# Rows of cumulated gates: spread over the partitions by DMA and masked on GpSimd, instead of by products on TensorE

## The chip, the cores and the metric

The kernel runs on one core of a Trainium2 chip. The metric is the device time of one execution in microseconds (us); three runs of the kernel before took 2589.52, 2592.03 and 2594.63 us, so the median is 2592.03 us. The engines are called as in the profile: PE (TensorE, matrix products), DVE (VectorE), ACT (ScalarE), POOL (GpSimd) and SP (SyncE, which here issues the weight loads).

## The reference

The model has two residual layers over 256 tokens of width 2048. The first mixes by centred means, the second by a gated delta rule in both directions; each has a cross-attention to 256 memory tokens, a SiLU gate and an output projection. What the change touches is in the second layer: the decay between two tokens of a chunk, for each of 32 heads and 2 directions, and its use in the triangular matrix and in the attention inside a chunk.

```python
g = jnp.cumsum(g.reshape(b, h, n, c), axis=-1)
tril = jnp.tril(jnp.ones((c, c), bool))
strict = jnp.tril(jnp.ones((c, c), bool), -1)
diff = g[..., :, None] - g[..., None, :]
decay = jnp.where(tril, jnp.exp(jnp.where(tril, diff, 0.0)), 0.0)
lower = jnp.where(strict, jnp.einsum('bhnid,bhnjd->bhnij', k_beta, k) * decay, 0.0)
a_mat = lower + jnp.eye(c, dtype=lower.dtype)
attn_intra = jnp.where(tril, jnp.einsum('bhnid,bhnjd->bhnij', q, k) * decay, 0.0)
```

## The kernel before

All dense products stream their weights: 802 tiles of 512 KB are loaded by SP into the buffers `wr` (`fetch`, line 208; `W_RAW_BUFS` of them), ACT makes the rounded high half `wh` (line 218), DVE the low half `wl` by a subtraction (line 220), each in one of three split buffers, and PE makes three products for each piece (high times high, high times low, low times high), into a bank called `pd`. `take` asks for the split of the tiles that come three later and for the loads that come `W_RAW_BUFS` after those. A tile's raw buffer is free when its subtraction has ended, a split buffer when PE has used the tile.

PE and SP issue in the order in which the class `Flow` writes the program. It keeps an estimated time `now`, adds to it for every product (in `mm`), and at each step of a dense job looks whether a chain (a Python generator that yields how long the other engines will need) is due; if so, the chain's next instructions are put there. DVE, ACT and POOL are ordered by a scheduler at build time, by priorities and by what is ready; each works through its own queue strictly in order.

The delta-rule layer has eight groups of four value heads. `group_chain(g)` makes, for each of two key heads, the gram matrix `kk` of the keys on PE, and then for its two value heads and two directions a pass:

- the cumulated gates of that head and direction, a row of 384 numbers (three blocks of 128 tokens), are spread over all 128 partitions by a product of a column of a selection matrix `selr` with `rows` (which holds the rounded value and its remainder in its two halves of the partitions); a second product, the identity `identr` with `maskr`, adds -1e30 where the decay has to vanish, in the first and the third block;
- ACT takes the exponentials of the sum with the bias `ngc` out of the PSUM bank `pa` into `Ap` (lines 936 and 937);
- DVE multiplies them with `kk` and a scalar into `U` (lines 940 and 945);
- the generator yields `Y_UA`.

Eight passes make a group, 64 the program. Afterwards DVE eliminates inside small blocks (lines 993 and 999, on `Ti`, whose start values POOL loads at line 913), PE puts the blocks together, `solve_pair` makes the outputs, and `norm_chain` and the gates finish the group while the next one's passes begin. `Ap` and `U` have one buffer each, so the passes of a group follow the last products that read the `Ap` of the group before.

`decay_chain` runs once, before the groups: it computes the gates, their cumulated rows `rowf` (64 heads and directions by 384), and splits them into `rows`. At the start of the program `mem_tiles` issues the first weight loads and the eight loads of the memory in turn, `fetch(c + 1 if c < W_RAW_BUFS else W_RAW_BUFS)` ahead of each.

Of the kernel before, what the change touches and what calls it, by code (L numbers as in the profile page):

```python
# [9 lines left out]
F32 = mybir.dt.float32  # L10
F32R = mybir.dt.float32r
I32 = mybir.dt.int32
AF = mybir.ActivationFunctionType
ALU = mybir.AluOpType
# [3 lines left out]
P = 128  # L18
S = 256
D = 2048  # L20
KT = D // P
# [5 lines left out]

# buffers per tag, and dense steps between two looks at the chains
W_RAW_BUFS = 4
W_SPLIT_BUFS = 3  # L30
PS_DENSE = 3
PS_CHAIN = 3
CHAIN_BUFS = 6
SQ_BUFS = 3
SLICE = 2
# priorities of the weight staging and of the parts of a chain on ScalarE and VectorE
P_STAGE = 600
P_UA = 600
P_INV = 600
P_NORM = 600  # L40
# how long the tensor engine leaves a step of a chain to the other engines, in units of US ns
US = 1300.0
# [20 lines left out]
CS_ID, CS_SEL, CS_ONE, CS_MASK = 0, 128, 192, 194  # L63
# [19 lines left out]
class Flow:  # L83
    """Interleaves dense weight products with the dependent chains, in the order the tensor engine issues them."""

# [52 lines left out]
def trunk_kernel(  # L138
# [18 lines left out]
    nc = tc.nc  # L157
    V, A, T = nc.vector, nc.scalar, nc.tensor
    flow = Flow()

    keep = ctx.enter_context(tc.tile_pool(name="keep", bufs=1))
# [8 lines left out]
    def pa(n):  # L170
        t = psa.tile([P, 512], F32, tag="a", name="pa")
        return t[:, 0:n]

    def mm(out, lhsT, rhs, start=True, stop=True):
        n = 1
        for d in rhs.shape[1:]:
            n *= d
        if rhs.dtype == F32R:
            flow.now += n / 2.4 if n >= 256 else n * 1.7
        elif lhsT.shape[0] == P:  # L180
            flow.now += 4 * n / 2.4 + 4
        else:
            flow.now += 2 * n / 2.4 + 4
        T.matmul(out, lhsT=lhsT, rhs=rhs, start=start, stop=stop)  # L184
# [494 lines left out]

    identr = keep.tile([P, P], F32R, name="identr")  # L680
    selr = keep.tile([P, 64], F32R, name="selr")
    maskr = keep.tile([P, 2, P], F32R, name="maskr")
    cwh = small[:, SM_CW : SM_CW + 320].rearrange("p (c k) -> p c k", k=5)
    nwh = keep.tile([P, 1], F32, name="nwh")
    fsel = keep.tile([P, 4], F32R, name="fsel")
    rows = keep.tile([P, 384], F32R, name="rows")
    ngc = keep.tile([P, 2, 64], F32, name="ngc")
# [6 lines left out]
    def decay_chain(ps):  # L694
        mask = mp.tile([P, 2, P], F32, tag="ms", name="mask", bufs=KT)
        nc.gpsimd.dma_start(out=mask, in_=cst_d[:, CS_MASK:CS_W].rearrange("p (d m) -> p d m", d=2))
        V.tensor_copy(out=identr, in_=ident)
        V.tensor_copy(out=selr, in_=cst[:, CS_SEL : CS_SEL + 64])
        V.tensor_tensor(
            out=fsel, in0=cst[:, CS_SEL : CS_SEL + 4], in1=cst[:, CS_SEL + 32 : CS_SEL + 36], op=ALU.add  # L700
        )
        V.tensor_copy(out=maskr, in_=mask)
        V.tensor_scalar(
# [48 lines left out]
        A.copy(out=rowf, in_=rps[0:64])  # L752
        A.copy(out=rows[0:64], in_=rowf)
        V.tensor_tensor(out=rows[64:128], in0=rowf, in1=rows[0:64].bitcast(F32), op=ALU.subtract)
        yield 1.5
# [17 lines left out]

    # second part: the jobs of the delta-rule groups
    kqs = [[None] * 4 for _ in range(8)]
# [115 lines left out]

    prio = [0]

    def urgent(gen, offset):
# [8 lines left out]
    def group_chain(g):  # L903
# [18 lines left out]
        for i in range(2):  # L922
            kk = gram(i, kq[i])
            for h in (2 * i, 2 * i + 1):
                for d in range(2):
                    hd = d * 4 + h
                    hdg = d * 32 + 4 * g + h
                    ja, jb = d, 1 - d
                    ps = pa(384)
                    mm(ps, selr[:, hdg : hdg + 1].to_broadcast([P, P]), rows, True, False)  # L930
                    mm(
                        ps.rearrange("p (b m) -> p b m", b=3)[:, 0:3:2, :], identr,
                        maskr[:, d : d + 1, :].to_broadcast([P, 2, P]), False, True,
                    )
                    E = Ap[:, hd, :]
# [452 lines left out]
```

## Time and profile before

| | |
|---|---|
| runs (us) | 2589.52, 2592.03, 2594.63 |
| profiled execution: span (us) | 2590.5 |
| profiled execution: time outside the span | not given by the profile |
| PE busy | 2566.3 us, 99% |
| DVE busy | 1788.2 us, 69% |
| ACT busy | 1238.0 us, 48% |
| POOL busy | 15.5 us, 1% |
| mean granted clock of PE | 0.998 |
| read from HBM | 430.63 MB, 167 GB/s over the span |

An engine is busy while at least one of its instructions runs. PE's matmuls overlap each other, so the duration of one is longer than the distance to the next; what a matmul takes from PE is that distance. Waits are listed as who waited, on which line, and what ended the wait.

### The profile page before, as it was taken

How to read it: one execution, taken by the hardware profiler on the slowest of the kernel's cores; microseconds unless marked ns; L12 is line 12 of the kernel's file. 1: busy time of each engine (PE TensorE's matmuls, PEld its weight loads, DVE VectorE, ACT ScalarE, POOL GpSimd, SP SyncE). 2: the span in 40 equal slices, each digit the busy share in tenths (PEclk: the TensorE clock that was granted, in tenths of full speed). 3: DMA queues.
4: the chain of work that ended last, by engine and by line, in shares of the span. 5: the costliest groups of instructions: out<-in, count | busy, mean ns of one | idle time of the engine just before them, and what ended most of it. 6: DMA issues, size and time to landing. Idle time of an engine off the chain costs nothing.

```text
span 2590.5 us, 53005 instructions
## 1 busy us (share of the span) xinstructions
PE 2566.3 (99%) x21996; PEld 2510.7 (97%) x21996; DVE 1788.2 (69%) x3317; ACT 1238.0 (48%) x1946; POOL 15.5 (1%) x44
## 2 busy tenths in 40 slices
PE   8999999999999999999999999999999999999998
PEld 7899999999999999998999999999999999999998
DVE  6564455656557576674546557989889797979786
ACT  5444434434444443554344445555545555565544
POOL 0000000000000000000000000000000000000000
PEclk9999999999999999999999999999999999999999
DMA  7654455555555555655554545535344454535353
GB/s 241 219 185 160 159 172 166 184 185 187 184 185 187 184 185 187 204 190 189 190 186 156 164 161 167 167 116 164 127 155 136 138 163 133 164 127 166 125 175 103
DMA packets 120817, 436.17 MB, mean 168 GB/s; under 512 B 13728, under 2 KB 13984, under 8 KB 120576
## 3 DMA queue, kind: packets, MB, share of 16 engines
q1 hardware_dynamic: 118080, 426.06, 50.4%
q0 software_dynamic: 1776, 5.64, 0.7%
q8 instruction: 172, 2.82, 0.4%
q10 hardware_dynamic: 720, 1.08, 0.1%
q14 instruction: 69, 0.57, 0.1%
HBM read 430.63 MB, written 2.10 MB: 167 GB/s over the span
## 4 chain that ended last, share of the span: by engine, by line
PE 96%; DVE 2%; ACT 1%; issue 0%; DMA 0%; POOL 0%; DVEq 0%
PE pd L184 86%; PE pa L184 9%; PE kk L184 1%; DVE wl L220 1%; PE pa L188 0%; ACT wh L218 0%; DMA xs<-in_mem_dram 0%; DVE ms L348 0%; DVE o L1264 0%; DMA wr<-in_wv_dram 0%; DVE Dg L983 0%; DVE cacc L795 0%; DVE L L985 0%; ACT ms L347 0%; DVE itmp L993 0%
## 5 line engine op out<-in xcount | busy, mean ns | idle before, releaser
L220 DVE TENSOR_TENSOR wl<-wr,wh 128x1024 fp32r<-128x1024 f32 x802 | 981.1, 1223 | 609.1 <-ACT wh L218 607.2
L184 PE MATMUL pd<-xs,wh 128*128 128x256 f32 x7328 | 1351.4, 286 | 2.8 <-DVE gt L411 2.1
L218 ACT CAST wh<-wr 128x1024 fp32r<-128x1024 f32 x802 | 841.0, 1049 | 1043.3 <-PE pd L184 839.8
L184 PEld LDWEIGHTS pd<-xs,wh 128*128 128x128 f32 x7328 | 1143.5, 192 | 7.4 <-DVE gt L411 2.3
L184 PE MATMUL pd<-xs,wl 128*128 128x256 f32 x3664 | 1036.5, 283 | 0.0
L184 PEld LDWEIGHTS pd<-xs,wl 128*128 128x128 f32 x3664 | 702.1, 192 | 0.0
L184 PE MATMUL pd<-y,wh 128*128 128x256 f32 x2944 | 524.0, 280 | 1.1 <-DVE y L258 1.1
L184 PEld LDWEIGHTS pd<-y,wh 128*128 128x128 f32 x2944 | 449.7, 187 | 1.8 <-DVE y L258 1.3
L184 PE MATMUL pd<-y,wl 128*128 128x256 f32 x1472 | 410.7, 279 | 0.0
L184 PEld LDWEIGHTS pd<-y,wl 128*128 128x128 f32 x1472 | 276.6, 188 | 0.0
L184 PE MATMUL pd<-ms,wh 128*128 128x256 f32 x1536 | 271.4, 279 | 0.0
L184 PEld LDWEIGHTS pd<-ms,wh 128*128 128x128 f32 x1536 | 234.8, 188 | 0.2
L184 PE MATMUL pd<-ms,wl 128*128 128x256 f32 x768 | 214.9, 280 | 0.0
L184 PE MATMUL pd<-wh,ms 128*128 128x512 f32 x512 | 163.4, 398 | 6.2 <-ACT ms L347 6.2
L184 PEld LDWEIGHTS pd<-ms,wl 128*128 128x128 f32 x768 | 144.3, 188 | 0.0
L795 DVE SCALAR_TENSOR_TENSOR cacc<-cu,small,cacc 128x256 f32<-128x256 f32 x256 | 122.5, 482 | 5.7 <-ACT cacc L793 1.3
L184 PEld LDWEIGHTS pd<-wh,ms 128*128 128x128 f32 x512 | 96.7, 189 | 29.2 <-ACT ms L347 6.2
L447 DVE TENSOR_TENSOR xT<-xT,pd 128x512 f32<-128x512 f32 x140 | 95.8, 684 | 41.2 <-PE pd L184 41.0
L184 PE MATMUL pd<-wl,ms 128*128 128x512 f32 x256 | 102.0, 398 | 0.3 <-DVE wl L220 0.2
L993 DVE TENSOR_TENSOR itmp<-L,Ti 128x126 f32<-128x126 f32 (+22 forms) x248 | 62.6, 252 | 2.3
L999 DVE TENSOR_TENSOR Ti<-Ti,itmp 128x126 f32<-128x126 f32 (+22 forms) x248 | 62.7, 253 | 2.2
L257 ACT CAST y<-yf 128x256 fp32r<-128x256 f32 x92 | 35.9, 405 | 55.7 <-DVE yf L525 54.0
(217 smaller groups left out, 1778.5 us busy)
## 6 DMA issues: line engine op xcount, KB each, us to landing
wr<-in_dw_dram SPq DMA_DIRECT2D x258, 512.0 KB, 3.5
wr<-in_pw_dram SPq DMA_DIRECT2D x192, 512.0 KB, 3.5
wr<-in_wo_dram SPq DMA_DIRECT2D x192, 512.0 KB, 3.5
wr<-in_wv_dram SPq DMA_DIRECT2D x64, 512.0 KB, 3.6
wr<-in_wk_dram SPq DMA_DIRECT2D x64, 512.0 KB, 3.5
wr<-in_pg_dram SPq DMA_DIRECT2D x32, 512.0 KB, 3.5
xs<-in_mem_dram SPq DMA_DIRECT2D x8, 256.0 KB, 7.1
xT<-in_x_dram SPq DMA_DIRECT2D x4, 512.0 KB, 6.3
```

Of the source, the lines that this page charges most:

```text
L184: T.matmul(out, lhsT=lhsT, rhs=rhs, start=start, stop=stop)
L218: A.copy(out=hi, in_=raw)
L220: V.tensor_tensor(out=lo, in0=raw, in1=hi.bitcast(F32), op=ALU.subtract)
L257: A.copy(out=dst[:, 0, :], in_=src)
L447: V.tensor_tensor(out=xv, in0=xv, in1=pss[0], op=ALU.add)
L795: V.scalar_tensor_tensor(out=a, in0=u[:, k : k + S], scalar=cwh[:, ct, k : k + 1], in1=a, op0=ALU.mult, op1=ALU.add)
L993: V.tensor_tensor(out=tv, in0=L[:, j + 1 : 32, j : j + 1].to_broadcast([P, n, c]), in1=Ti[:, j : j + 1, 0:c].to_broadcast([P, n, c]), op=A ...
L999: V.tensor_tensor(out=Ti[:, j + 1 : 32, 0:c], in0=Ti[:, j + 1 : 32, 0:c], in1=tv, op=ALU.subtract)
```

## The change

The rows stay in float32 and are written once to DRAM, to `rows_d`, by a DMA from POOL. For each pass a DMA from POOL reads the one row of 1536 bytes 128 times, into one of four buffers `er`, and POOL adds the mask to its first and third block. `fetch_rows` asks for the rows of the passes up to four ahead (`ROW_BUFS`), over the borders of groups. ACT takes the exponentials out of `er`. The two products, the casts to `identr`, `selr` and `maskr` and the split into `rows` are gone, and the mask stays in a buffer of its own. There are three raw weight buffers, where there were four. (The diff also takes out some comments.)

```diff
-W_RAW_BUFS = 4
+
+W_RAW_BUFS = 3
 W_SPLIT_BUFS = 3
 PS_DENSE = 3
 PS_CHAIN = 3
 CHAIN_BUFS = 6
+ROW_BUFS = 4
...
-    identr = keep.tile([P, P], F32R, name="identr")
-    selr = keep.tile([P, 64], F32R, name="selr")
-    maskr = keep.tile([P, 2, P], F32R, name="maskr")
+    mask = keep.tile([P, 2, P], F32, name="mask")
+    dram = ctx.enter_context(tc.tile_pool(name="dram", bufs=1, space=bass.MemoryType.DRAM))
+    rows_d = dram.tile([64, 384], F32, name="rows_d")
...
-        A.copy(out=rows[0:64], in_=rowf)
-        V.tensor_tensor(out=rows[64:128], in0=rowf, in1=rows[0:64].bitcast(F32), op=ALU.subtract)
+        nc.gpsimd.dma_start(out=rows_d, in_=rowf)
...
+    order = [(g, i, h, d) for g in range(8) for i in range(2) for h in (2 * i, 2 * i + 1) for d in range(2)]
+    ahead = []
+
+    def fetch_rows(n):
+        while len(ahead) < min(n, len(order)):
+            g, _, h, d = order[len(ahead)]
+            hdg = d * 32 + 4 * g + h
+            er = gpool[0].tile([P, 384], F32, tag="er", name="er", bufs=ROW_BUFS)
+            nc.gpsimd.dma_start(out=er, in_=rows_d[hdg : hdg + 1, :].to_broadcast([P, 384]))
+            ends = er.rearrange("p (b m) -> p b m", b=3)[:, 0:3:2, :]
+            nc.gpsimd.tensor_tensor(
+                out=ends, in0=ends, in1=mask[:, d : d + 1, :].to_broadcast([P, 2, P]), op=ALU.add
+            )
+            ahead.append(er)
...
-                    ps = pa(384)
-                    mm(ps, selr[:, hdg : hdg + 1].to_broadcast([P, P]), rows, True, False)
-                    mm(
-                        ps.rearrange("p (b m) -> p b m", b=3)[:, 0:3:2, :], identr,
-                        maskr[:, d : d + 1, :].to_broadcast([P, 2, P]), False, True,
-                    )
+                    n = order.index((g, i, h, d))
+                    fetch_rows(n + ROW_BUFS)
+                    ps, ahead[n] = ahead[n], None
```

On PE, at the start of the passes of the sixth group (`kk<-kq` is the gram matrix, `pd<-xs` the dense products), the order before was:

```order
L184 MATMUL pd<-xs,wl 128x256
L184 MATMUL kk<-kq 128x256
L184 MATMUL kk<-kq 128x128 x2
L184 MATMUL pa<-rows,selr 128x384
L184 MATMUL pa<-maskr,identr 128x2x128
L184 MATMUL pd<-xs,wh 128x256 x2
L184 MATMUL pd<-xs,wl 128x256
```

The same place on PE now:

```order
L185 MATMUL pd<-xs,wl 128x256
L185 MATMUL kk<-kq 128x256
L185 MATMUL kk<-kq 128x128 x2
L185 MATMUL pd<-xs,wh 128x256 x2
L185 MATMUL pd<-xs,wl 128x256
```

The two products of the pass are gone and the dense products follow the gram matrix at once; the same number of dense rows as before stands between the two gram matrices of a group.

On ACT, at the same group's passes (`ot` is an output of the group before, `wh` a weight cast, `Ap` the exponentials), the order before was:

```order
L1177 COPY ot<-pa 128x512
L1180 ACTIVATE osq<-ot 128x512
L799 ACTIVATE th<-cacc 128x256
L218 CAST wh<-wr 128x1024
L936 ACTIVATE Ap<-pa,ngc 128x256
L937 ACTIVATE Ap<-pa,ngc 128x128
L218 CAST wh<-wr 128x1024
L792 COPY cu_17327<-pd 128x256
L936 ACTIVATE Ap<-pa,ngc 128x256
L937 ACTIVATE Ap<-pa,ngc 128x128
```

The same place on ACT now:

```order
L942 ACTIVATE Ap<-er,ngc 128x256
L1186 ACTIVATE osq<-ot 128x512
L219 CAST wh<-wr 128x1024
L943 ACTIVATE Ap<-er,ngc 128x128
L942 ACTIVATE Ap<-er,ngc 128x256
L943 ACTIVATE Ap<-er,ngc 128x128
L942 ACTIVATE Ap<-er,ngc 128x256
L943 ACTIVATE Ap<-er,ngc 128x128
L219 CAST wh<-wr 128x1024
L942 ACTIVATE Ap<-er,ngc 128x256
L943 ACTIVATE Ap<-er,ngc 128x128
```

The exponentials of one pass after another stand close together, right behind the last output of the group before; only weight casts lie between them.

On ACT at the start of the program (`ms` are the scaled memory tiles, `sq` squares), the order is now:

```order
L219 CAST wh<-wr 128x1024
L348 ACTIVATE ms<-xs,small 128x256 x12
L280 ACTIVATE sq<-xs 128x256 x2
L219 CAST wh<-wr 128x1024
```

The first of these casts is that of the third weight tile, the second that of the fourth, which stood ahead of the last ten `ms` before.

## Rows read from the trace of the kernel before

**Rows 1.** The head of the profile page: span, busy time of each engine.

```profile
span 2590.5 us, 53005 instructions
PE 2566.3 (99%) x21996; PEld 2510.7 (97%) x21996; DVE 1788.2 (69%) x3317; ACT 1238.0 (48%) x1946; POOL 15.5 (1%) x44
```

**Rows 2.** The page's chain that ended last, by engine.

```profile
PE 96%; DVE 2%; ACT 1%; issue 0%; DMA 0%; POOL 0%; DVEq 0%
```

**Rows 3.** Waits of PE, by line: us in total, times, longest.

```profile
PE pa L188 <- DVE itmp L993: 2.2, 1, 2.2
PE pd L184 <- DVE gt L411: 2.1, 1, 2.1
PE pa L184 <- ACT frow L1122: 1.4, 1, 1.4
```

**Rows 4.** One group's stretch: length; PE, PEld, DVE, ACT, POOL busy; clock; DMA share; GB/s.

```profile
2307.94:2425.56 117.62, 117.62 (x1169) 116.45 (x1167) 101.55 (x252) 64.64 (x119) 0.54 (x1) 1.00 0.45 146
```

**Rows 5.** PE's timeline at one pass: start, duration, instruction.

```profile
1605.34 0.34 PE L184 MATMUL pa<-rows,selr 128*128 128x384 f32 x1
1605.51 0.28 PE L184 MATMUL pa<-maskr,identr 128*128 128x256 f32 x1
1605.63 0.40 PE L184 MATMUL pd<-xs,wh 128*128 128x256 f32 x2
```

**Rows 6.** Instructions on the tile rows: count, min/median/max ns, first and last start.

```profile
L184 PE MATMUL pa<-rows,selr x64: 337/338/423, 1602.1 to 2448.0; 128*128 128x384 f32 x64
```

**Rows 7.** Waits of ACT and of SP's queue.

```profile
ACT wh L218 <- PE pd L184: 839.8, 512, 4.0
...
SPq L208 <- DVE wl L220: 1187.2, 428, 8.4
```

**Rows 8.** Timelines of ACT and DVE around one weight tile.

```profile
502.83 1.05 ACT L218 CAST wh<-wr 128x1024 fp32r<-128x1024 f32 x1 [1.78 <-PE pd L184]
505.61 1.05 ACT L218 CAST wh<-wr 128x1024 fp32r<-128x1024 f32 x1 [1.74 <-PE pd L184]
...
503.91 1.23 DVE L220 TENSOR_TENSOR wl<-wr,wh 128x1024 fp32r<-128x1024 f32 x1 [1.60 <-ACT wh L218]
```

**Rows 9.** DMA issues: queue, count, KB each, median us from issue to landing.

```profile
wr<-in_dw_dram SPq DMA_DIRECT2D x258, 512.0 KB, 3.5
...
xs<-in_mem_dram POOLq DMA_DIRECT2D x8, 256.0 KB, 8.0
Ti<-in_t_dram POOLq DMA_DIRECT2D x8, 256.0 KB, 2.9
...
cum<-in_cum_dram POOLq DMA_DIRECT2D x4, 192.0 KB, 5.3
```

**Rows 10.** Timelines at the start: SP's queue, ACT, DVE, PE.

```profile
4.86 2.97 SPq L327 DMA_DIRECT2D xs<-in_mem_dram  x5
12.73 4.11 ACT L347 ACTIVATE ms<-xs,small 128x256 fp32r<-128x256 f32 x10
...
16.70 0.40 PE L184 MATMUL pd<-wl,ms 128*128 128x512 f32 x1
...
18.63 1.22 DVE L220 TENSOR_TENSOR wl<-wr,wh 128x1024 fp32r<-128x1024 f32 x1
```

**Rows 11.** Groups by line and shape on DVE and POOL: count | busy us, mean ns.

```profile
L220 DVE TENSOR_TENSOR wl<-wr,wh 128x1024 fp32r<-128x1024 f32 x265 | 323.6, 1221 | 69.3 <-ACT wh L218 67.8 <-issue 0.3
L280 DVE TENSOR_TENSOR acc<-acc,sq 128x256 f32<-128x256 f32 x13 | 5.5, 422 | 1.5 <-ACT sq L279 1.0
...
L913 POOL DMA_DIRECT2D Ti<-in_t_dram x8 | 4.3, 536 | 1094.2 <-PE pa L184 581.9 <-issue 268.1 <-ACT th L409 244.2
...
L1238 POOL MEMSET frow<- 128x256 f32 x1 | 0.3, 335 | 0.0
```

**Rows 12.** Groups by line and shape on ACT: the exponentials.

```profile
L936 ACT ACTIVATE Ap<-pa,ngc 128x256 f32<-128x256 f32 x64 | 30.3, 473 | 21.9 <-PE pa L184 21.4
L937 ACT ACTIVATE Ap<-pa,ngc 128x128 f32<-128x128 f32 x64 | 23.1, 362 | 0.0
```

More of the change, by code (lines that the diff above doesn't have):

```diff
@@ L685, in trunk_kernel @@
     fsel = keep.tile([P, 4], F32R, name="fsel")
-    rows = keep.tile([P, 384], F32R, name="rows")
     ngc = keep.tile([P, 2, 64], F32, name="ngc")
@@ L694, in decay_chain @@
     def decay_chain(ps):
-        mask = mp.tile([P, 2, P], F32, tag="ms", name="mask", bufs=KT)
         nc.gpsimd.dma_start(out=mask, in_=cst_d[:, CS_MASK:CS_W].rearrange("p (d m) -> p d m", d=2))
-        V.tensor_copy(out=identr, in_=ident)
-        V.tensor_copy(out=selr, in_=cst[:, CS_SEL : CS_SEL + 64])
         V.tensor_tensor(
@@ L701, in decay_chain @@
         )
-        V.tensor_copy(out=maskr, in_=mask)
         V.tensor_scalar(
```

## The prediction

> **What bounds the kernel now.** I read the page's busy times first: TensorE (PE) is busy 2566.3 of 2590.5 us, VectorE (DVE) 69%, ScalarE (ACT) 48% [rows 1]. The page's chain of waits says the same from the end backwards: 96% of the span lies on PE [rows 2]. Then the waits of PE alone: in the part that the change touches, three of any size, 2.2, 2.1 and 1.4 us, 5.7 us together [rows 3]; in a late group of the delta rule (117.62 us) PE is busy all of it, but DVE is too for 101.55 us [rows 4]. So an instruction taken from PE's queue shortens the run by its own pitch, as long as DVE, ACT and the weight stream still keep ahead of PE. The rest asks whether they do.
>
> **What is removed.** The 64 passes (8 groups, 2 head pairs, 2 heads, 2 directions) each lose a 384-column and a 256-column product. PE overlaps matmuls, so the 338 ns duration of the first [rows 6] is not its price; the distance to the next start is. One pair starts at 1605.34, its second product at 1605.51, the next dense product at 1605.63 [rows 5]: 0.17 + 0.12 = 0.29 us. 64 x 0.29 = 18.6 us, all on the path. The one-time casts and the split of the rows (four DVE, one ACT) lie beside a full PE and count nothing. Elsewhere PE's order moves by a few rows only.
>
> **What is added on the path of the exponentials.** Each pass now needs a DMA of 192 KB from DRAM and one GpSimd addition over 256 elements. Four rows are held ahead. At a group's start four are ready long before; the row for pass n+4 is asked for when ACT has done the exponentials of pass n. The trip back is an issue of 0.54 us [rows 11], a landing, and the addition. For the landing the nearest row is the 256 KB one on the same queue in the same part of the program, 2.9 us; four loads in a burst took 5.3, eight beside the x and weight traffic 8.0 [rows 9]. For the addition no row exists: DVE takes 0.42 us for an addition of this size, 1.22 us for one four times as long [rows 11]; I take 0.5, bounds 0.3 (GpSimd's own memset of 256 elements is 0.34 us [rows 11]) and 1.2. Trip: 0.54 + 2.9 + 0.5 = 3.9 us, bounds 3.7 and 9.7. What ACT has queued between the end of exponentials n and the start of n+4 are three pairs (0.47 + 0.36 us each [rows 12]) and by the order one weight cast of about 1.05, 3.5 us, and that cast waits for PE besides. So ACT waits 0.4 us at most in the central case.
>
> Behind such a wait in ACT's queue stand weight casts, and PE waits for those. Their lead: there are three split buffers, and a cast starts when PE leaves one (840 us of ACT's waits are this [rows 7]). PE then has two tiles of 2.8 us ahead; cast and subtraction are done 503.91 + 1.23 - 502.83 = 2.3 us after the cast began [rows 8]. 5.6 - 2.3 = 3.3 us of lead. A trip hurts PE only beyond 3.5 + 3.3 = 6.8 us; the bound of 9.7 would cost 2.9 us in each of 8 groups, 23 us, the central case nothing.
>
> The page of the Trainium skill titled "SBUF — State Buffer" (section "A bandwidth-pool intuition that's wrong (but worth ruling out)") says that DMAs issued from GpSimd starve for descriptors while DVE runs an instruction that uses both of its ports, and gives about 620 ns alone against 3100 ns beside one. This trace speaks against it for our place: the loads of the same queue landed in 2.9 us with DVE busy 86% of the time [rows 4, 9]. By the page's figure the trip would be an estimated 6.4 us, still under 6.8.
>
> **What is added on DVE's side.** By the order, DVE makes the same instructions but forms the eight U of a head pair in a burst instead of pass by pass, so the elimination starts earlier against PE. That can only remove waits of PE (at best the 5.7 us). Against it stands the addition on GpSimd. With 8 additions a group of at most 1.2 us, and DVE held for all of each, DVE goes from 101.6 to 111.2 us of a group that shrinks to 117.6 - 8 x 0.29 = 115.3: full to 96%, not over. I put 1 us in the sum for it, my choice nearest to the late groups, where PE has no such wait [rows 3, 4]; bounds -5.7 (the three waits vanish) and +9.5 (the second rival below).
>
> The same page, section "Who interferes with whom", states that a DVE instruction with two SBUF inputs and a GpSimd instruction that reads SBUF exclude each other for the length of the one that came first. No run here shows GpSimd arithmetic. By that rule the holding of DVE assumed above is what happens; without it the term would be 0.
>
> **Three raw buffers instead of four.** The load queue waits for the subtraction to give a buffer back (1187 us in all [rows 7]), so one buffer fewer makes each load start one tile later. Given back 2.3 us after its cast began, landed 3.5 us later [rows 9], that is 5.8 us; the cast it serves begins four tiles later now, 11.2 us, and three tiles later after the change, 8.4 us. 2.6 us of spare are left, and PE's 3.3 us behind that. In the delta-rule part tiles follow each other more slowly and the spare is larger. Cost nothing, except where there is no lead yet:
>
> **The start.** The fourth weight load stood among the first mem loads; now it stands behind all eight, whose issue ends at 4.86 + 2.97 = 7.83 us. By ACT's order its cast falls behind all twelve mem scalings and two squares. The last ten scalings end at 12.73 + 4.11 = 16.84 us [rows 10]; take away the 1.03 of the cast that leads them now, add 0.7 for two squares, and the cast ends near 17.2 us with its subtraction at about 18.4. PE's first product with that tile's low half is at 16.70 us [rows 10]. Loss 1.7 us; bounds 0 (data and ACT ahead as now) and 19.85 - 16.70 = 3.2 us (the tile comes when now the fifth does, whose subtraction runs from 18.63 for 1.22 [rows 10]).
>
> **Sum.** Against the profiled execution: 2590.5 - 18.6 + 1.7 + 1 = 2574.6 us. Page and trace give no time outside the span; the median of the runs is 2592.03, 1.5 us above, so I add that: **2576 us**. Bounds of the terms: 1.7 + 5.7 lower at the one end gives 2592.0 - 18.6 - 5.7 = 2567.7; at the other the rivals.
>
> **Rivals.**
> *DVE late.* GpSimd's additions fall among DVE's and PE meets in each of the eight groups a wait like those of the first groups, 5.7 / 3 = 1.9 us: 8 x 1.9 = 15.2 instead of 5.7, 9.5 more than now: 2592.0 - 18.6 + 1.7 + 9.5 = 2585 us. For it: DVE at 86% with hardly any slack after the change. Against: in the last groups there is no such wait at the same load [rows 3, 4], and the burst gives the chain lead.
>
> *Rows late at the head of ACT's queue; slower than before.* One mechanism: the trip of a refill is so long that exponentials 5 to 8 of each group stop ACT with casts behind. It decides from 6.8 us on, and turns the sign where it eats the gain: (18.6 - 1.7) / 8 = 2.1 us a group, at a trip of 8.9. At 11.4 us (the 8.0 landing, four issues of 0.54, 1.2 of addition) it is 4.6 x 8 = 37 us: 2592.0 - 16.9 + 37 = 2612 us; at the bound of 9.7, 2598. For it: bursts on this queue have taken 5.3 and 8.0. Against: those were four and eight loads at once, here refills leave one by one, and 192 KB per 3 us adds little to DMA engines that are busy 45% [rows 4].
>
> *The gain is given back.* The products leave PE, but its order was spaced with their time in it, and PE stands where they were. 2592 + 1.7 = 2594 us. Against: between the two grams of a group PE still has the same dense rows, back to back, and the inputs of what follows come earlier.
>
> **How the numbers follow.** About 0.2% (5 us) is what a measurement of this kernel can tell from no change: faster is below 2587, slower above 2597. Forecast 0.72, DVE late 0.13, rows late 0.10, given back 0.05. The forecast is all faster; DVE late splits 0.08 faster, 0.04 same, 0.01 slower; rows late 0.02 same, 0.08 slower; given back 0.04 same, 0.01 slower. Faster 0.80, same 0.10, slower 0.10. The forecast alone has 2568 to 2583; the range takes in the second case and the edge of the others: 2567 to 2592.
>
> **What would show it.** Right: no products from rows and maskr on PE, 64 additions on GpSimd, the groups' pitch near 115.3 us, PE still busy throughout a group, a landing of the rows near 3 us, and one wait of PE of 1 to 3 us for the low half before 25 us. Wrong: waits of PE for wl or wh in the first 15 us of each group with ACT waiting for the exponentials' input (rows late); the fixed-size DVE instructions longer than 0.48 and 1.22 us beside GpSimd's (DVE held); casts that wait for the weight DMA (three buffers too few).

## The result: slower by 2.4%, and the profile after

The changed kernel took 2652.1 us (median of four runs, 2651.15 to 2655.24), the kernel before 2591.06 in runs beside it: ratio 1.0235, with a 95% interval of 1.0221 to 1.025. The forecast was 2576 us, faster. The head of the page and its chain of waits, which answer to [rows 1, 2]:

```profile
span 2653.3 us, 52948 instructions
PE 2566.0 (97%) x21868; PEld 2507.1 (94%) x21868; DVE 1807.0 (68%) x3313; ACT 1245.5 (47%) x1945; POOL 109.2 (4%) x173
...
PE 91%; DVE 5%; DMA 1%; ACT 1%; issue 1%; POOL 1%; DVEq 0%; SPq 0%; ACTq 0%; POOLq 0%
```

128 products are gone (21996 to 21868), and yet PE is busy for as long as before. The chain now lies on DVE for 5%. The waits of PE, in us in total, times and longest, answer to [rows 3]:

```profile
PE pa L189 <- DVE itmp L999: 40.6, 6, 8.0
PE pa L189 <- DVE fcol L1121: 8.4, 5, 3.5
PE pa L185 <- ACT sq L817: 6.1, 2, 3.9
...
PE pa L189 <- DVE xn L795: 5.7, 1, 5.7
...
PE pd L185 <- ACT wh L219: 1.6, 1, 1.6
...
PE pd L185 <- DVE wl L221: 1.1, 1, 1.1
```

The first line is new in size: 2.2 us became 40.6. Line 189 is the transpose helper, and the place is the same in each late group: the transposes of a value head. The group from one such wait to the next, and the first stretch behind the wait (length; PE, PEld, DVE, ACT, POOL busy; clock; DMA share; GB/s), answer to [rows 4]:

```profile
2120.38:2247.10 126.72, 117.43 (x1149) 115.90 (x1149) 104.71 (x252) 66.02 (x120) 12.14 (x17) 0.97 0.48 148
2255.10:2261.00 5.90, 5.90 (x37) 5.90 (x38) 5.88 (x23) 3.16 (x7) 0.00 (x0) 0.70 0.00 0
```

A group takes 126.7 us where it took 117.6, and 115.3 were forecast. PE stands for 9.3 us of it, and in the first 5.9 us behind the wait its granted clock is 0.70 in the mean. PE's timeline at that place (start, duration, instruction, in brackets the wait before it):

```profile
2246.58 0.40 PE L185 MATMUL pd<-xs,wh 128*128 128x256 f32 x2
2246.82 0.28 PE L185 MATMUL pd<-xs,wl 128*128 128x256 f32 x1
2255.02 0.66 PE L189 MATMUL pa<-cst,xn 128*128 128x128 f32 x2 [7.92 <-DVE itmp L999]
2255.34 0.78 PE L185 MATMUL pd<-xs,wh 128*128 128x256 f32 x2
2255.91 0.41 PE L185 MATMUL pd<-xs,wl 128*128 128x256 f32 x1
2256.12 0.63 PE L185 MATMUL pd<-xs,wh 128*128 128x256 f32 x2
```

Ahead of the wait the dense products start 0.12 us apart (two of them from 2246.58 to 2246.82), behind it 0.21 (2255.91 to 2256.12): the granted clock is at the lower of its two levels, 1.2 GHz. So there are two losses, the standing and the slow work behind it. The releaser is named as `itmp`, but the tile waited for is `xn`, and `xn` is where to look on DVE:

```profile
2234.09 0.47 DVE L790 SCALAR_TENSOR_TENSOR cacc<-cu,small,cacc 128x256 f32<-128x256 f32 x1
...
2245.90 0.33 DVE L951 SCALAR_TENSOR_TENSOR U<-kk,sk,Ap 128x128 f32<-128x128 f32 x1
2246.16 1.21 DVE L221 TENSOR_TENSOR wl<-wr,wh 128x1024 fp32r<-128x1024 f32 x1
2247.30 1.78 DVE L989 STREAM_TRANSPOSE Dg<-U 32x256 f32<-32x256 f32 x4
2249.11 0.48 DVE L790 SCALAR_TENSOR_TENSOR cacc<-cu,small,cacc 128x256 f32<-128x256 f32 x1
2249.51 1.22 DVE L221 TENSOR_TENSOR wl<-wr,wh 128x1024 fp32r<-128x1024 f32 x1
2250.64 1.90 DVE L991 STREAM_TRANSPOSE L<-Dg 128x1024 f32<-128x1024 f32 x1
2252.46 0.45 DVE L790 SCALAR_TENSOR_TENSOR cacc<-cu,small,cacc 128x256 f32<-128x256 f32 x1
...
2254.45 0.42 DVE L795 SCALAR_TENSOR_TENSOR xn<-th,cacc 128x256 f32<-128x256 f32 x1
```

DVE is not slow here, it works without a break; it works on something else. While PE stands from 2247.1, DVE turns `Dg` and `L` for an elimination that PE needs much later, and the convolution of the value head (`cacc`, `xn`) comes behind it. Its input had been there for long: the first of its steps ran at 2234.09, the next step of any convolution at 2249.11. On ACT, from the end of the group before (`ot`), where [rows 12]'s exponentials once waited for PE 21.4 us in all:

```profile
2220.33 0.59 ACT L1183 COPY ot<-pa 128x512 f32<-128x512 f32 x1 [2.83 <-PE pa L185]
2220.81 0.51 ACT L942 ACTIVATE Ap<-er,ngc 128x256 f32<-128x256 f32 x1
...
2227.95 0.51 ACT L942 ACTIVATE Ap<-er,ngc 128x256 f32<-128x256 f32 x1 [0.18 <-POOL er L898]
2228.37 0.39 ACT L943 ACTIVATE Ap<-er,ngc 128x128 f32<-128x128 f32 x1
2228.66 0.36 ACT L787 COPY cu<-pd 128x256 f32<-128x256 f32 x1
2228.92 0.48 ACT L788 ACTIVATE cacc<-pd,small 128x256 f32<-128x256 f32 x1
```

The same engine in the kernel before, at the end of a group:

```profile
2299.73 0.37 ACT L792 COPY cu<-pd 128x256 f32<-128x256 f32 x1
2299.99 0.48 ACT L793 ACTIVATE cacc<-pd,small 128x256 f32<-128x256 f32 x1
2301.54 0.59 ACT L1177 COPY ot<-pa 128x512 f32<-128x512 f32 x1 [1.07 <-PE pa L184]
...
2308.52 0.47 ACT L936 ACTIVATE Ap<-pa,ngc 128x256 f32<-128x256 f32 x1 [0.96 <-PE pa L184]
```

In after the exponentials no longer wait for PE. The scheduler that orders ACT and DVE at build time therefore sees them ready as soon as `Ap` is free, and their priority is high (600): five pairs stand ahead of the first copy `cu` of a value convolution, which before stood ahead even of `ot`. From that copy to the end of `xn` it takes 26.2 us here (2228.66 to 2254.87), where the kernel before took 5.9 (2299.73 to 2305.60). The same then happens on DVE with `U` and the start of the elimination.

For every run below I worked the profiled span out in three parts from the trace: the gaps of PE over 0.25 us; the loss at 1.2 GHz (half of PE's busy time in stretches with that granted clock, without the start and the last 20 us); and the rest, which is what PE would need at full clock without standing. The parts are those of the one profiled execution, and the loss is an estimate: by the distances of 0.21 and 0.12 us it would be 43% instead of half, 15 us instead of 17.4 in after. Each ratio is to runs of the kernel before that were made beside it.

| kernel | median us | ratio to before (95%) | PE stands | lost at 1.2 GHz | rest |
|---|---|---|---|---|---|
| before | 2592.0 | | 8.4 | 1.7 | 2580.4 |
| after | 2652.1 | 1.0235 (1.0221 to 1.025) | 72.1 | 17.4 | 2563.9 |
| passes_low | 2621.4 | 1.011 (1.0095 to 1.0125) | 39.9 | 14.4 | 2565.5 |
| conv_first | 2624.0 | 1.0124 (1.0109 to 1.0139) | 43.3 | 19.4 | 2563.2 |
| transposes_late | 2627.8 | 1.0137 (1.012 to 1.0154) | 42.4 | 14.5 | 2568.3 |
| spaced | 2634.4 | 1.0158 (1.0143 to 1.0174) | 49.8 | 15.4 | 2566.7 |
| exp_tied | 2634.9 | 1.016 (1.0145 to 1.0175) | 36.7 | 14.7 | 2582.4 |
| exp_tied_spaced | 2608.0 | 1.0059 (1.0043 to 1.0076) | 14.1 | 5.1 | 2584.1 |
| norm_first | 2605.2 | 1.0044 (1.0029 to 1.0059) | 27.5 | 6.4 | 2565.7 |
| passes_low_add2 | 2654.7 | 1.0237 (1.0222 to 1.0252) | 61.0 | 22.6 | 2566.2 |
| passes_low_nomask | 2616.9 | 1.0099 (1.0075 to 1.0122) | 33.6 | 16.7 | 2565.5 |
| passes_low_dmamask | 2648.1 | 1.0213 (1.0197 to 1.0228) | 56.8 | 23.6 | 2564.5 |
| norm_first_nomask | 2592.2 | 1.0001 (0.9991 to 1.001) | 19.7 | 9.7 | 2564.0 |
| norm_first_dmamask | 2617.2 | 1.0092 (1.0077 to 1.0107) | 36.2 | 14.0 | 2565.5 |
| norm_first_rows6 | 2603.2 | 1.0044 (1.0028 to 1.006) | 24.7 | 14.8 | 2561.8 |
| norm_first_late_fcol | 2602.7 | 1.0043 (1.0028 to 1.0058) | 27.8 | 6.5 | 2567.6 |
| half_rows | 2623.7 | 1.0122 (1.0107 to 1.0137) | 31.1 | 18.4 | 2574.2 |
| half_rows_norm_first | 2605.3 | 1.0048 (1.0032 to 1.0065) | 19.2 | 12.6 | 2574.7 |
| before_raw3 | 2594.1 | 1.0007 (0.9998 to 1.0017) | 11.0 | 3.3 | 2580.7 |
| before_close | 2595.2 | 1.0011 (1.0002 to 1.0021) | 9.4 | 3.4 | 2581.2 |

The rest of after is 16.5 us below that of before (14 with the smaller estimate of the loss): the gain of the removed products is there. It is buried under 63.7 us more of standing and 15.7 us more at the lower clock.

### The profile page after: what moved, and what is told of

Read it like the earlier page. It is cut to its first block, busy times and chain, and to the rows that moved or that the text cites. A ratio compares the mean times of both kernels' runs of the same rounds, so it can differ in the third digit from the quotient of the medians.

```text
span 2653.3 us, 52948 instructions
## 1 busy us (share of the span) xinstructions
PE 2566.0 (97%) x21868; PEld 2507.1 (94%) x21868; DVE 1807.0 (68%) x3313; ACT 1245.5 (47%) x1945; POOL 109.2 (4%) x173
## 4 chain that ended last, share of the span: by engine, by line
PE 91%; DVE 5%; DMA 1%; ACT 1%; issue 1%; POOL 1%; DVEq 0%; SPq 0%; ACTq 0%; POOLq 0%
PE pd L185 82%; PE pa L185 8%; DVE wl L221 1%; PE kk L185 1%; DVE cacc L790 1%; DMA er<-rows_d 1%; PE pa L189 1%; DVE L L991 1%; DVE Dg L989 0%; ACT wh L219 0%; POOL er L898 0%; DVE U L946 0%; DMA xs<-in_mem_dram 0%; DMA wr<-in_wv_dram 0%; DVE U L951 0%
```

## The experiments

Theory 1 is the order just read. Its rivals: additions on GpSimd hold DVE (theory 2); three raw buffers, or the traffic of the rows (theory 3); and, added after the first four runs, that PE's steps of the chain now follow each other too closely (theory 4).

**conv_first, passes_low: the order alone**

```diff
 # conv_first
+                with tc.high_priority(offset=P_STAGE):
                     conv_silu(ps, 32 + 4 * g + n, 4 + n, vc)
 # passes_low
-P_UA = 600
+P_UA = 0
```

> The changed kernel; only the build-time priority of the convolution of a value head (the cacc steps, tanh and xn behind a v job) is raised by 600, to that of the weight staging and of the chain. All 64 GpSimd additions, the row transfers, the three raw buffers and PE's order stay. Theory 1 (VectorE's queue: the U of a head pair and the start of the elimination are now ready at once, so the build-time scheduler puts them ahead of the value convolutions, and PE stands 7 to 8 us a group at the transposes of those): the wait of PE at the v transposes is gone, no half-clock stretch follows, time 2575 to 2590 us. Theory 2 (GpSimd's additions hold VectorE): the same 64 additions fall on the same engine, time stays above 2630 us. Theory 3 (three raw buffers, or the row transfers beside the weights): above 2630 us too.

> The changed kernel; only the raised build-time priority of the passes (exponentials and U) is set from 600 to 0. Theory 1 (VectorE's queue order): the convolutions of the value heads move ahead of the U of the same time, PE's wait at the v transposes is under 1 us a group, time 2575 to 2590 us. Theory 2 (GpSimd's additions hold VectorE): above 2630 us. Theory 3 (raw buffers, row transfers): above 2630 us.

Both are 28 to 31 us faster than after and below the 2630 us of theories 2 and 3, so the order is a cause; both are far above the 2590 us that theory 1 gave at most, so it is not the only one. The waits of PE in conv_first, then in passes_low:

```profile
PE pa L189 <- DVE fcol L1122: 32.3, 7, 6.3
...
```

```profile
PE pa L189 <- DVE fcol L1121: 15.1, 7, 2.7
PE pa L185 <- DVE N L1009: 10.5, 6, 2.3
PE pa L185 <- DVE NT L1013: 7.4, 6, 1.5
```

The wait at the transposes is gone from both lists and another stands in its place: `fcol`, the end of the normalisation, or `N`, the end of the elimination.

**transposes_late: PE asks later**

```diff
-Y_VT = 15.61
+Y_VT = 22.0
```

> The changed kernel; only the spacing on PE between a value convolution's dense product and its transposes is lengthened from 15.61 to 22 units (of 1.3 us), so PE asks for xn some 8 us later. Theory 1: PE meets xn ready, no wait of 7 us a group and no half-clock stretch, 2575 to 2605 us (the later values may delay the solve a little). Theory 2 and 3: VectorE or the weight stream is late as a whole, so the wait turns up elsewhere; above 2630 us.

24 us faster than after, but above the expected 2575 to 2605 us: the transposes find `xn` ready, and PE waits instead for the gates (`gt`, 22.6 us in seven waits).

**before_raw3: the buffers**

```diff
 # in the kernel before
-W_RAW_BUFS = 4
+W_RAW_BUFS = 3
```

> The kernel before with three raw weight buffers instead of four, nothing else. Theories 1 and 2: only the start changes, 1 to 3 us more for one wait of PE on the low half of the fourth weight tile; 2592 to 2595 us. Theory 3 (the buffers make the loss): 2620 us or more.

1.0007 with 1 in the interval. In the kernel before, three buffers cost nothing that can be measured; theory 3 falls as far as the buffers go by themselves. The changed kernel with four was not run.

**exp_tied, exp_tied_spaced, spaced, before_close: the released exponentials and the spacing**

```diff
 # exp_tied
+                    bs = pa(2)
+                    mm(bs, ident, ngc[:, :, hdg])
+                    nb = wt([P, 2], F32, "nb2", 4)
+                    A.copy(out=nb, in_=bs)
...   # and bias=nb[:, 0:1], bias=nb[:, 1:2] in the exponentials
 # exp_tied_spaced: exp_tied and this; spaced: after and this
-Y_UA = 1.8
+Y_UA = 2.01
 # before_close: the kernel before and
-Y_UA = 1.8
+Y_UA = 1.59
```

> The changed kernel, but each pass's exponentials wait for PE again: a tiny product of the identity with the two bias columns of the pass stands on PE where the two large products stood, ScalarE copies its two columns and the exponentials take their bias from the copy. Rows by DMA, GpSimd additions and three raw buffers stay. In the program order ScalarE's copies for the value convolutions stand ahead of the exponentials again. Theory 1 (the released exponentials, a burst of 13 at the head of a group on ScalarE, and the U behind them push the value convolutions back): no wait at the v transposes over 1 us, time below 2600 us. Theory 2 (GpSimd's additions hold VectorE, some 2.6 us of busy time a group): at least 2592 us with waits on N or fcol. Theory 4 (PE's steps of the chain now follow each other 8 x 0.29 us sooner in a group, and VectorE's chain had only 1.8 to 2.8 us to spare at N and fcol): waits of 1 to 3 us at N or fcol, 2590 to 2605 us. All of it harmless: 2580 us.

> As exp_tied, and the spacing of the passes on PE is lengthened from 1.8 to 2.01 units of 1.3 us, which gives each pass the 0.27 us back that its two products took in PE's written order (the dense products in between are then more, the total is the same). Theory 4 (the lost spacing): the waits of PE at N and fcol that exp_tied has go, 2577 to 2590 us. Theory 2 (GpSimd's additions hold VectorE): waits stay, no gain over exp_tied of more than 5 us.

> The changed kernel, only the spacing of the passes on PE from 1.8 to 2.01 units of 1.3 us. Theory 4 (lost spacing takes VectorE's chain its slack): most of the loss goes, below 2615 us. Theory 1 (released exponentials and U stand ahead of the value convolutions): the burst stays, PE still waits several us a group for xn, above 2630 us.

> The kernel before, only the spacing of the passes on PE from 1.8 to 1.59 units of 1.3 us: PE's steps of the chain follow each other 8 x 0.27 us sooner in a group, as in the changed kernel, with the products, the exponentials' wait for PE and no GpSimd additions. Theory 4: PE waits of 1 to 3 us at N, fcol or xn in each group, with half-clock stretches behind the longer ones, 2600 to 2625 us. If the spacing has slack: within 5 us of 2592 us.

exp_tied came out far above what theories 1 and 4 gave. Its tiny products cost PE as much as the removed ones had (rest 2582.4), so read the standing: 36.7 us instead of 72.1, but not 8.4 as before. The largest part is now at the gates (`gt`, 16.5 us); 6.5 us are left at `xn`, of 46.3. With the spacing given back it is 14.1, and the time falls by 27 us, more than theory 2 alone allowed; it stays above theory 4's range by about what the tiny products cost. Without the tie, the spacing alone (spaced) leaves 49.8, and its 2634.4 us lie above the 2615 that theory 4 gave. In the kernel before, the same shortening of the spacing costs at most 0.2%, far less than theory 4 expected. So the lost 0.27 us a pass makes the loss larger, it doesn't start it. That it hurts where the chain on DVE is late already fits these four runs, but no run isolates it.

**norm_first: order and spacing together**

```diff
-P_UA = 600
+P_UA = 0
-P_NORM = 600
+P_NORM = 1200
-Y_UA = 1.8
+Y_UA = 2.01
```

> The changed kernel with the passes at priority 0, the normalisation of the outputs at 1200 instead of 600, and the passes' spacing on PE at 2.01 instead of 1.8. Theories 1 and 4 together: fcol comes earlier than in passes_low, the wait for it goes (15 us in all there), the waits at N (18 us in all) shrink, 2580 to 2600 us. Theory 2 (GpSimd's additions): waits move to N, above 2605 us.

47 us faster than after, and on the border between the two expectations; the waits at `N` are gone. PE waits for `fcol`:

```profile
PE pa L189 <- DVE fcol L1121: 16.7, 7, 7.8
```

The first two groups have 7.8 and 4.2 us of it. In the first the timeline of POOL and that of DVE (start, duration) read side by side:

```profile
1725.29 0.72 POOL L898 TENSOR_TENSOR er<-er,mask 128x256 f32<-128x256 f32 x1 [3.68 <-DMA er<-rows_d]
1725.95 0.55 POOL L896 DMA_DIRECT2D er<-rows_d  x1
1726.61 0.71 POOL L898 TENSOR_TENSOR er<-er,mask 128x256 f32<-128x256 f32 x1
```

```profile
1725.02 0.16 DVE L271 SCALAR_TENSOR_TENSOR nu<-nu,so 128x8 f32<-128x8 f32 x1
1725.10 0.34 DVE L951 SCALAR_TENSOR_TENSOR U<-kk,sk,Ap 128x128 f32<-128x128 f32 x1
1725.36 0.67 DVE L272 SCALAR_TENSOR_TENSOR ny<-nu,ny 128x8 f32<-128x8 f32 x1
...
1726.68 0.67 DVE L271 SCALAR_TENSOR_TENSOR nu<-nu,so 128x8 f32<-128x8 f32 x1
1729.12 1.23 DVE L221 TENSOR_TENSOR wl<-wr,wh 128x1024 fp32r<-128x1024 f32 x1 [1.77 <-ACT wh L219]
```

An operation on 8 elements takes 0.16 us, and 0.67 when it starts 0.07 us after an addition on POOL: it ends when that ends. The normalisation is a chain of such small operations, so an addition of 0.7 us that falls on one of them lengthens it by 0.5. That is the rule of the Trainium skill's page "SBUF — State Buffer" (section "Who interferes with whom") that the prediction cited: two SBUF inputs on DVE and a reading GpSimd exclude each other. Here the trace agrees. The last line shows the other half of the price: DVE stands 1.77 us for a weight cast that stood on ACT behind exponentials, which waited 2.07 us for their row, up to 1726.04.

**The additions: 128, 64, none, and by DMA**

```diff
 # passes_low_add2: passes_low, the addition twice
 # passes_low_nomask, norm_first_nomask: no addition (decay and mask are left out of the result), and
+ A.activation(out=E[:, 0:256], in_=ps[:, 0:256], func=AF.Exp, scale=1e-3)
+ A.activation(out=E[:, 256:384], in_=ps[:, 256:384], func=AF.Exp, scale=1e-3)
 # passes_low_dmamask, norm_first_dmamask
-            nc.gpsimd.tensor_tensor(
-                out=ends, in0=ends, in1=mask[:, d : d + 1, :].to_broadcast([P, 2, P]), op=ALU.add
-            )
+            nc.gpsimd.dma_start(
+                out=ends,
+                in_=cst_d[:, CS_MASK + d * P : CS_MASK + d * P + P][:, None, :].to_broadcast([P, 2, P]),
+                accum_op=ALU.add,
+            )
```

> As passes_low, and GpSimd makes each addition of the mask twice (128 instead of 64; the sum stays far below what the exponential can tell from zero). VectorE's order is the same, row by row, as in passes_low, so the difference to its 2621 us is the price of 64 more additions. Theory 2 (the additions hold VectorE, which is late in each group): 8 x 2.6 = 21 us more or above, 2635 to 2660 us. Theory 1 and 4 (order and spacing alone): within 5 us of 2621 us.

> As passes_low, but the additions of the mask are left out altogether, and so that the numbers stay finite the exponentials are taken of a thousandth of the rows without the bias (same two instructions of the same size): decay and mask are left out of the result. Theory 2 (additions hold VectorE): 64 added cost 33 us, so 64 taken away give 20 to 33 us back, 2588 to 2601 us, with cacc at 480 ns and the 8-element operations at 164 ns. Theory 1 and 4 alone: 2616 to 2626 us. If the trip of the rows were what costs, the wait of ScalarE for er shrinks by the addition's own 0.75 us a row only, and the time stays above 2610 us.

> As passes_low, but the mask is added by an accumulating DMA from DRAM into the first and third block instead of by a GpSimd instruction; no GpSimd arithmetic is left. VectorE's order is the same row by row. 64 more additions cost 33 us (passes_low_add2 against passes_low). Theory 2 (each addition holds VectorE about as much): taking 64 away gives 25 to 33 us back, 2588 to 2597 us, and cacc, U and yf beside them have their plain lengths. Theory 1 and 4 alone (order and spacing): within 5 us of passes_low's 2621 us, the waits at N and fcol stay. A refill that is late with two transfers in a row shows as ScalarE waiting for er over 2 us.

> As norm_first, with the additions left out and the exponentials of a thousandth of the rows without the bias, as in passes_low_nomask: decay and mask are left out of the result. Theories 1, 2 and 4 together: order, spacing and hold remedied, 2575 to 2590 us, below before; the remaining waits are those for er at the first groups. If it stays above 2595 us, a fourth part (trip of the rows) is still in the loss.

> As norm_first (passes at priority 0, normalisation at 1200, spacing 2.01), with the mask added by an accumulating DMA instead of by GpSimd. If order, spacing and the held VectorE (theories 1, 4 and 2) are all of the loss, the three remedies together bring the gain of the change out: before less 20 us of products plus 2 to 3 us at the start and some us in the first group, 2572 to 2588 us, below the kernel before. If something else is in the loss (raw buffers, row traffic): 2592 us or more.

DVE's order in passes_low, passes_low_add2 and passes_low_dmamask is the same but for one `wl` that changes places with a `cacc` near. In the two kernels without the addition it is not: there DVE has the same instructions, but some of them stand elsewhere, around the passes (the traces differ in some 60 places from passes_low to passes_low_nomask), and ACT's order differs too. The heads of the pages of passes_low_nomask, passes_low and passes_low_add2:

```profile
PE 2566.2 (98%) x21868; PEld 2506.9 (96%) x21868; DVE 1778.9 (68%) x3313; ACT 1229.2 (47%) x1945; POOL 50.1 (2%) x109
```

```profile
PE 2563.8 (98%) x21868; PEld 2504.7 (96%) x21868; DVE 1804.9 (69%) x3313; ACT 1242.9 (47%) x1945; POOL 119.1 (5%) x173
```

```profile
PE 2572.5 (97%) x21868; PEld 2512.3 (95%) x21868; DVE 1835.5 (69%) x3313; ACT 1241.9 (47%) x1945; POOL 165.6 (6%) x237
```

The same 3313 instructions of DVE take 26.0 us longer with 64 additions and 30.6 us more with the next 64: 0.41 and 0.48 us held for each. That settles that theory 2's mechanism is real. Its price in time is clear in one pair, where DVE's order stays: the second 64 cost passes_low_add2 33 us. With the first 64, passes_low is 4.5 us above passes_low_nomask (the intervals of the two overlap), and norm_first 13 us above norm_first_nomask; in both pairs the order moves too, and how much of the difference is the hold alone was not separated. I had expected 20 to 33 us from passes_low_nomask, and there it missed. That PE pays only once DVE's chain has no slack left would fit, and is not shown. norm_first_nomask ends where before does, just above the 2575 to 2590 us expected. In a late stretch it shows what had been forecast:

```profile
2280.00:2396.00 116.00, 116.00 (x1156) 114.71 (x1155) 103.17 (x253) 63.99 (x120) 4.79 (x9) 1.00 0.52 163
```

PE never stands, at full clock. From PE's first product with `N` in one group to that in the next, the third to the sixth of the seven distances are 115.5 us, against 115.3 forecast, 116.2 to 118.3 in before and 126.4 to 128.2 in after. The first two are 118.6 and 121.3 (116.0 and 120.0 in before). There PE stands for `fcol`:

```profile
PE pa L189 <- DVE fcol L1116: 9.3, 2, 5.7
```

With the additions these two waits were 7.8 and 4.2 us, without them (and with the order moved) they are 5.7 and 3.5: the hold can be only the smaller part of them. The row traffic is in this kernel too; with whatever else is left it eats the gain of 16 us and no more.

The two runs by DMA missed altogether, and are of use for another rival, that of the prediction in which the rows come late. DVE was as free as without additions (1778.5 us busy on its page), yet the time rose by 27 and 12 us. Landings of the row and of the mask, then ACT's and PE's waits, in passes_low_dmamask:

```profile
er<-rows_d POOLq DMA_DIRECT2D x64, 192.0 KB, 5.0
er<-in_cst_dram POOLq DMA_DIRECT2D x64, 128.0 KB, 5.7
```

```profile
ACT Ap L944 <- DMA er<-in_cst_dram: 55.9, 25, 7.5
...
PE pa L185 <- ACT frow L1130: 18.1, 5, 7.4
```

The view counts a landing from the start of its issue, so the trip is at least 5.0 + 5.7 = 10.7 us, and exponentials stop ACT with work for PE behind them: that is the rival's mechanism. But the weight casts that it named are the smaller part. PE waits 7.7 us for `wh` and 3.8 for `wl` (2.3 and 2.6 in passes_low_nomask), and 18.1 for `frow`, another cast of ACT (10.4). The rival gave 37 us for a trip of 11.4, by its sum 31 for 10.7; against passes_low_nomask the DMA costs 31, and that the two agree is partly luck.

**norm_first_rows6, norm_first_late_fcol: what is left of norm_first**

```diff
 # norm_first_rows6: norm_first and
-ROW_BUFS = 4
+ROW_BUFS = 6
-CHAIN_BUFS = 6
+CHAIN_BUFS = 5
 # norm_first_late_fcol: norm_first and
-ROW_BUFS = 4
+ROW_BUFS = 5
-Y_FAC = 5.08
+Y_FAC = 6.4
```

> As norm_first, with six row buffers instead of four (and five instead of six of the small chain buffers, to make room), so that of eight rows of a group only two are on their way while ScalarE works. Trip of the rows a part of the loss: ScalarE's waits for er (2.1 us at the longest in norm_first) and with them the waits of PE for fcol in the first groups shrink, 2585 to 2600 us. Hold of VectorE alone: within 4 us of 2605 us.

> As norm_first, with five row buffers and the wait of PE for fcol moved 1.7 us later in its written order (5.08 to 6.4 units). The waits for fcol (16.7 us in norm_first, 7.8 and 4.2 us of it in the first two groups) go to 8 us or less, 2590 to 2598 us; if VectorE's chain is late as a whole, the wait turns up at N or at the v transposes and the time stays within 4 us of 2605 us.

Neither differs from norm_first by what the runs can tell (2603.2 and 2602.7 against 2605.2). With six buffers ACT's waits for rows fall from 20.8 us to 0.5, and PE's for `fcol` do not (16.7 and 18.7): once order and spacing are mended, the trip of the rows is no part of the loss that can be measured. Moving PE's point made other waits (`NT`, `wl`) out of a part of those for `fcol`, as transposes_late had.

**half_rows, half_rows_norm_first: half of the change**

```diff
-    order = [(g, i, h, d) for g in range(8) for i in range(2) for h in (2 * i, 2 * i + 1) for d in range(2)]
+    order = [(g, i, h, d) for g in range(8) for i in range(2) for h in (2 * i, 2 * i + 1) for d in (1,)]
...
+                    if d == 1:
                         n = order.index((g, i, h, d))
                         fetch_rows(n + ROW_BUFS)
                         ps, ahead[n] = ahead[n], None
+                    else:
+                        ps = pa(384)
+                        mm(ps, selr[:, hdg : hdg + 1].to_broadcast([P, P]), rows, True, False)
...   # and the product with maskr, as before; Y_UA = 1.9; CHAIN_BUFS = 5
 # half_rows_norm_first: and P_UA = 0, P_NORM = 1200
```

> The changed kernel for one direction only: of the eight passes of a group four (direction 1) take their row by DMA with the addition on GpSimd, four (direction 0) by the two products on PE as before; all four rows of a group are on the chip before its passes begin. Spacing 1.9 instead of 1.8 units, five small chain buffers instead of six. 32 additions instead of 64, and half the exponentials wait for PE again. Theories 1 and 2 (released exponentials, held VectorE): half of the products' 22 us is gained, the v transposes wait less than half as much as in the changed kernel: 2590 to 2615 us. If only the refills on their way during the passes cost: 2582 to 2588 us.

> As half_rows, with the passes at priority 0 and the normalisation at 1200 as in norm_first. Theories 1 and 2 with their remedies on half of the passes: 2580 to 2592 us, at or below the kernel before; if VectorE's chain has no room for any of it: 2595 to 2605 us.

With half the additions and no wait of ACT for a row, half_rows still loses 32 us to before, more than expected, and the priorities alone give 18 of it back. No version beat the kernel before; the best that computes the reference, norm_first_late_fcol, is 0.4% above it.

## Why the prediction was wrong

**The step that failed** is this one: DVE "forms the eight U of a head pair in a burst instead of pass by pass, so the elimination starts earlier against PE. That can only remove waits of PE (at best the 5.7 us)." The first half came true. In the seventh group `N`, the elimination's end, began 17.7 us before PE's first use of it, against 3.6 before; PE's own stand of 7.9 us at `xn`, in which DVE went on, is in that lead (timeline of DVE, then of PE, of after):

```profile
2420.25 1.21 DVE L1009 STREAM_TRANSPOSE N<-Ti 128x512 f32<-128x512 f32 x1
```

```profile
2437.93 0.21 PE L185 MATMUL pa<-N,U 32*32 32x32 f32 x1
```

The second half does not follow. On an engine that works strictly in order, work that comes earlier puts other work later, and I did not ask which. The order of DVE and ACT was there to be compared: the exponentials stood ahead of `cu`, and `U`, `Dg` and `L` ahead of the `cacc` and `xn` that PE takes next. Priorities that had been harmless while the exponentials waited for PE became an order in which PE stands 46.3 us for `xn` (40.6 + 5.7). passes_low shows it by one number changed: the wait for `xn` is gone, and 31 of the 61 us come back.

**The gain was right.** 64 x 0.29 = 18.6 us were forecast; the rest of the table fell by 16.5 in after and by 12 to 19 in every version without the products (exp_tied has tiny ones in their place). The rival "the gain is given back" did not come.

**GpSimd's hold was mis-sized, and its effect mis-placed.** I put 1 us in the sum and 9.5 us as a bound ("DVE late", 2585 us). DVE is held 26 us in all (passes_low against passes_low_nomask), 3.3 us a group, within the bound that I had worked out for the hold (9.6 us a group); but I took the late groups' lack of waits as room. What it costs in time is shown by the second 64 in passes_low, 33 us; for the first 64 the runs give between 4.5 and 13, with the order moved as well.

**What a wait costs was left out.** Every rival was priced by the waits alone. Behind its longer waits PE ran at the lower level; in after that adds 15.7 us to 63.7. The trace of before has one such stretch in its groups, 3.4 us.

**The trip of the rows** was forecast at 3.9 us with bounds of 3.7 and 9.7. As the landing of 2.9 holds the issue already, that sum counted the issue twice and should have been 3.4. The landing took 4.2 us (median) and the addition 0.93 (mean); from the start of the issue to the end of the addition the 64 trips of after take 5.4 us in the median, 7.8 at most, so most are under the 6.8 from which it was to hurt. ACT waits 18.1 us for it in 23 times, 1.9 at most, where the forecast had 0.4. It is no main part, as forecast. In the first group it has a share: `sq` ran on ACT at 1585.31, 8.4 us after its input was done, behind exponentials that had waited 1.9 and 1.4 us for rows, and PE stood 2.3 us for it. passes_low, with the same rows and another order, has no such wait.

**Three raw buffers and the start**: forecast nothing but 1.7 us at the start, 3.2 at most. before_raw3 is 1.0007 (0.9998 to 1.0017), and in after PE's start waits are 1.6 + 1.1 us, against 0.2 in before. Right in size; the wait for `wh` among them was not foreseen.

**What stays open.** norm_first_nomask has order, spacing and hold mended, without computing the reference, and stands at before's time, not 16 us under it. In its profiled execution PE stands 11.3 us more and loses 8 us more to the clock than in before; 9.3 us of the standing is at `fcol` in the first two groups. I found no order in which these two run as the late ones do. In the first, the trace shows DVE standing 2.0 us within that wait for a weight cast that stood on ACT behind exponentials, which had waited 0.9 and 1.4 us for rows; why the normalisation is latest in these two groups was not tried by itself. So the order is shown as the largest cause, the hold as a real one; how the rest divides stays open.

## What to carry to other kernels

Taking a dependency away is a change of order too: before pricing it, look on every in-order engine at what the freed work now stands ahead of, and at which of that another engine takes next. That an engine is busy only 86% does not say that the chain through it has slack; price what the freed work displaces, add what the clock loses behind a wait of PE, and set priorities and spacing anew together with the change. An addition moved to GpSimd is not free for VectorE: here each one held it for about 0.4 us.

## What the hardware showed

- In after a GpSimd addition of 128x256 takes 0.71 to 0.74 us where no instruction of DVE overlaps it, 0.93 in the mean and up to 1.78; DVE's 8-element operations take 0.15 to 0.17 us by themselves and up to 0.98 beside it.
- At the lower level of the granted clock dense products start 0.21 us apart, at the higher 0.12.
- A row of 1536 bytes spread over 128 partitions (192 KB) landed 4.2 us after the start of its issue (median of after); an accumulating DMA of 128 KB from DRAM took 5.7 (passes_low_dmamask).
